# Seven products instead of eight in the mixers' second gates and in retention's output product

## The chip, the cores and the metric

The kernel runs on one core of one Trainium2 chip. The metric is the device time of one execution in microseconds (us). Of the kernel before there are three runs: 2315.1, 2315.0 and 2314.92 us, median 2315.0 us.

## The reference, cut to what matters

One decoder layer on 256 tokens of width 2048, in float32. Two half feed-forward blocks stand around a pair of token mixers that work side by side, and a gated embedding follows. The change touches the mixers only:

```python
rq, rk, rv, rg, aq, ak, av, gate_r, gate_a = jnp.split(h @ w_in[i], SPLIT_POINTS, axis=-1)
...
ro = head_group_norm(retention_chunkwise(rq, rk, rv), ret_gn_g[i]).astype(h.dtype)
ret_branch = (jax.nn.silu(rg) * ro) @ w_ret_out[i]
...
att_branch = sliding_window_attention_sinks(aq, ak, av, att_sinks[i]) @ w_att_out[i]

mixed = (jax.nn.sigmoid(gate_r) * ret_branch + jax.nn.sigmoid(gate_a) * att_branch) @ w_mix_out[i]
```

`gate_r`, `gate_a`, `w_ret_out` and `w_mix_out` are 2048 by 2048; `w_att_out` is 1024 by 2048, since attention has 16 heads of 64.

## The kernel before, in words

Every float32 product is made of three matmuls. A weight chunk of 128 x 1024 floats (512 KB) is loaded by the queue of SyncE (line 105), ACT rounds it to a high part (line 91), DVE subtracts to get the low part (line 92), and PE adds low x high, high x high and high x low into one PSUM bank (lines 291 to 293, in `Sum.add`). The activations are split into high and low parts in the same way. A chunk that covers 512 columns and two blocks of 128 rows of the weight ("a single") feeds two token halves, so it costs PE 2 x 2 x 3 = 12 matmuls of 128 x 512.

The feed-forward blocks already use a second form. `Seven` takes the two chunks of one pair of row blocks for two neighbouring column blocks, and treats tokens x rows times rows x columns as a product of 2 x 2 blocks, which is done with seven products in place of eight (a scheme of Strassen's kind). PE runs 7 x 3 = 21 matmuls where two singles take 24. For that DVE makes four sums of weight blocks (lines 163 to 166) and three and a half low parts of 1024 where two singles need two; ACT rounds three and a half times. The left side needs sums of the activations as well (`seven_forms`, lines 362 to 365, and a split). At the end of a column pair a fold of four additions (lines 373 to 376) joins the common products, and four more additions (line 794 in the feed-forward) join the plain ones. `block` runs such a column pair: a list of units, "P" for a pair of singles and "S" for a seven, with four PSUM banks for the plain sums and four for the common ones, eight in all, which is the whole PSUM.

All instructions are recorded in program order and each engine runs its own in that order. `plan` is the list of all weights in the order of use. `fill` runs ahead of PE: it loads and splits weights as long as less than `ahead` = 45 matmuls of work lie ready, fewer than 90 are loaded, and the count of buffers that the stage granted (`slots_for_weights`) is not used up. A single holds two of these buffers, a seven holds seven and needs eight while it is made. There are 46 in all, and the activations lie in the same pool. Smaller work (the heads of retention and attention, transposes) stands in the list `side`; one entry is run after each unit of weights (`run_side`).

In the mixers the order is: retention's values, queries and keys, retention's gate (tiles `rg`), attention's queries and keys (`aqk`, five groups of four chunks), attention's values (`av`), then the second gates (`gt`, eight blocks of 512 columns with eight singles each). While the `gt` blocks run, the side list takes the eight pairs of attention heads, each in four parts: scores `att1` (tiles `as`, DVE maxima), exponentials `att1b` on ACT, scaling `att1c` on DVE, transposes `att2` (tiles `at`), and the product with the values `att3` (tiles `ao`, then `attt`). ACT copies each gate out of PSUM (`sig`, line 1182). Then for each of four column blocks come retention's output product (`mr`, eight singles) and attention's (`ma`, four singles); DVE multiplies each by its gate (lines 1207, 1211), adds them (1212), and the sum is transposed into `mixt` (line 1198) for the last product (`mo`).

Of the kernel before, what the change touches and what calls it, by code (L numbers as in the profile page):

```python
# [15 lines left out]
P = 128  # L16
# [32 lines left out]
def layer(ctx: ExitStack, tc: tile.TileContext, io):  # L49
# [13 lines left out]
    def banks(name):  # L63
        return [bank(name + str(j)) for j in range(2)]
# [290 lines left out]
    def seven_forms(full, hi, lo):  # L355
# [10 lines left out]
        split(hi, lo, raw)  # L366
        return lambda e: [(hi[:, 2 * j + e, :], lo[:, 2 * j + e, :]) for j in range(4)]

    def seven_common(p1, p6, p7, q5):

        e, w = slot([P, 2, 512], F32, "eve"), slot([P, 2, 512], F32, "evw")
        act.copy(e[:, 0], p1)
        dve.tensor_tensor(w[:, 0], e[:, 0], p6, ALU.add)
# [315 lines left out]
    def gu_units(j):  # L689
        if j == 0:  # L690
            return [("P", p) for p in range(KD // 2)]
        order = "PPSSPSSP" if j % 2 == 0 else "PPSPSPSP"
        sevens = list(SEVEN[: order.count("S")])
        plain = [p for p in range(KD // 2) if p not in sevens]
        return [(kind, (sevens if kind == "S" else plain).pop(0)) for kind in order]

    def gu_keys(name, j):
        return lambda n, p: (name + "_gu", j, n, p)
# [198 lines left out]
    def plan_mixers():  # L897
        plan_tokens(("w_rv", 0), KD)
        for grp in range(8):
            plan_features([("w_in_f", grp)], KD)  # L900
        for blk in range(1, 4):
            plan_tokens(("w_rv", blk), KD)
        for grp in range(8, 16, 2):
            plan_tokens(("w_in_f2", grp), KD)
        for grp in range(16, 21):
            plan_features([("w_in_f", grp)], KD)
        plan_tokens(("w_av",), KD, nk=4)
        for grp in range(21, 37, 2):
            plan_tokens(("w_in_f2", grp), KD)
        for j in range(0, 8, 2):  # L910
            plan_tokens(("w_ret2", j), KD)
            plan_tokens(("w_att2", j), KD // 2)
        for blk in range(4):
            plan_tokens(("w_mix", blk), KD)

# [6 lines left out]
    def mixers(ht, norm, residual, keepers, away):  # L922
# [142 lines left out]
        for j in range(5):  # L1065
            ps = banks(f"aqk{j}")
            features_out([(("w_in_f", grp), ps)], KD, both_halves)
            grp += 1
            dst = akv[:, 0:2, :] if j == 4 else aq[j // 2][:, j % 2 * 2 : j % 2 * 2 + 2, :]
            rotate(ps, f"ra{j}", dst, cos_a, sin_a, SH_A)  # L1070
# [4 lines left out]
        assert not side or len(side) < 3  # L1075
        run_side(len(side))

        att_t = []

        def att1(m):  # L1080
            def f():
                c = m // 4
                q, k = aq[c][:, m % 4, :], akv[:, c, :]
                ps = banks(f"as{m}")
                for e in range(2):
                    r = slice(e * DH, (e + 1) * DH)
                    pe.matmul(ps[e][:, :P], q[r, :P], k[r, :P], start=True, stop=True)
                    pe.matmul(ps[e][:, P:384], q[r, P:], k[r, :], start=True, stop=True)
# [12 lines left out]
                es = small.tile([P, 2, 2], F32, tag="aes", name=f"aes{m}")  # L1101
                dve.tensor_tensor(es, skb, mx, ALU.subtract)
                keep["a", m] = s, nm, es
            return f

        def att1b(m):
            def f():
                s, nm, es = keep["a", m]
                act.activation(es, es, AF.Exp)
                sm = small.tile([P, 2, 2], F32, tag="asm", name=f"asm{m}")  # L1110
                for t in range(2):
                    for e in range(2):
                        x = s[:, e, :P] if t == 0 else s[:, e, P:]
                        act.activation(
                            x, x, AF.Exp, bias=nm[:, t, e : e + 1], accum_out=sm[:, t, e : e + 1]
                        )
                keep["b", m] = sm
            return f

        def att1c(m):  # L1120
            def f():
                (s, nm, es), sm = keep.pop(("a", m)), keep.pop(("b", m))
                dve.tensor_tensor(sm, sm, es, ALU.add)
                dve.reciprocal(sm, sm)
                for t in range(2):
                    for e in range(2):
                        x = s[:, e, :P] if t == 0 else s[:, e, P:]
                        dve.tensor_scalar(x, x, sm[:, t, e : e + 1], None, ALU.mult)
                keep["p", m] = s
            return f  # L1130
# [14 lines left out]
        def att3(m):  # L1145
# [16 lines left out]
                    dve.tensor_tensor(d[r, S:], ps[e][r, :S], d[r, :S], ALU.subtract)  # L1162
# [12 lines left out]
        sig = []  # L1175
        for j in range(8):
            ps = banks(f"gt{j}")
            paired_out(("w_in_f2", grp), KD, rhs, ps)
            grp += 2
# [3 lines left out]
        run_side(len(side))  # L1183

        mix_t = []
        y = {}
# [5 lines left out]
        def turned(v, kk):  # L1192
# [5 lines left out]
                    pe.transpose(ps[:, j, t * P : (t + 1) * P], v[:, t, (kk + j) * P : (kk + j + 1) * P], ident)  # L1198
            split(mt[:, :, :S], mt[:, :, S:], ps)

        for j in range(4):
            for v in (sig[j], sig[4 + j]):
                act.activation(v, v, AF.Sigmoid)
            pr = banks(f"mr{j}")
            paired_out(("w_ret2", 2 * j), KD, lambda k: of_pairs(ret_t, k), pr)
            for t in range(2):
                dve.tensor_tensor(sig[j][:, t], sig[j][:, t], pr[t], ALU.mult)
            pa = banks(f"ma{j}")
            paired_out(("w_att2", 2 * j), KD // 2, lambda k: of_pairs(att_t, k), pa)
            for t in range(2):  # L1210
                dve.tensor_tensor(sig[4 + j][:, t], sig[4 + j][:, t], pa[t], ALU.mult)
            dve.tensor_tensor(sig[j], sig[j], sig[4 + j], ALU.add)
            later(1, lambda v=sig[j]: turned(v, 0))
            later(2, lambda v=sig[j]: turned(v, 2))

        stats = small.tile([P, 2, 4, 6], F32, tag="stats", name="mixst", bufs=1)

# [232 lines left out]
```

## Time and profile before

| what | us |
|---|---|
| median of three runs | 2315.0 |
| the profiled execution | 2312.8 |
| its span, first to last instruction | 2311.0 |
| PE busy | 2279.6 |
| DVE busy | 1871.4 |
| ACT busy | 1162.9 |

The profiled execution is 2.2 us shorter than the median. Its span leaves out 1.8 us before the first and after the last instruction. Busy time of an engine is the time in which at least one of its instructions was running; PE's matmuls overlap, so a busy PE says that it never stood still, and not how many matmuls it could have done. The stages of the change lie between 1072.3 us (first `gt` matmul) and 1402.9 us (first `mo` matmul).

### The profile page before, as it was taken

What the parts mean: (1) busy time and instruction counts of PE and PEld (TensorE: products, weight loads), DVE (VectorE), ACT (ScalarE), POOL (GpSimd) and SP (SyncE); (2) the same over time, 40 slices, a digit from 0 to 9 for tenths busy, and PEclk for the clock granted to TensorE, in tenths of its full rate; (3) what the DMA queues carried; (4) which work ended last, traced back from release to release, by engine and by line L of the source; (5) the groups of instructions that cost most, each with busy time, mean ns of one, the idle gap of its engine ahead of it and who ended that gap; (6) DMA issues with size and microseconds to landing.
All of it is one profiled execution on the core that took longest, in us unless ns stands there. A gap on an engine that the chain in (4) does not pass through costs nothing.

```text
span 2311.0 us, 28634 instructions
## 1 busy us (share of the span) xinstructions
PE 2279.6 (99%) x10502; PEld 1887.7 (82%) x10502; DVE 1871.4 (81%) x2348; ACT 1162.9 (50%) x1404; POOL 97.0 (4%) x53
## 2 busy tenths in 40 slices
PE   9999999999999999999999999999999999999997
PEld 7788888888887888888778888888888888888876
DVE  7999999988988874677655555779999999889876
ACT  5555555565553342434554543355565555655432
POOL 0000000000000530133000000000000000000000
PEclk9999999999999999999999999999999999999999
DMA  9566666665587565546556667476666566565771
GB/s 316 164 218 191 194 208 194 197 218 182 201 287 263 176 225 160 170 150 198 159 158 183 184 207 260 161 249 207 192 191 212 182 204 217 172 219 193 289 255 55
DMA packets 193725, 465.70 MB, mean 202 GB/s; under 512 B 14768, under 2 KB 16048, under 8 KB 193584
## 3 DMA queue, kind: packets, MB, share of 16 engines
q1 hardware_dynamic: 191456, 460.91, 60.7%
q10 hardware_dynamic: 2128, 2.97, 0.4%
q8 instruction: 82, 1.34, 0.2%
q14 instruction: 59, 0.48, 0.1%
HBM read 455.43 MB, written 8.39 MB: 201 GB/s over the span
## 4 chain that ended last, share of the span: by engine, by line
PE 95%; DVE 3%; issue 1%; DMA 0%; ACT 0%; DVEq 0%; ACTq 0%
PE f2g L293 3%; PE f2g L291 3%; PE f2g L292 3%; PE f1g L291 3%; PE gt L291 3%; PE f1g L292 3%; PE f1g L293 3%; PE rqk L242 3%; PE gt L292 3%; PE gt L293 3%; PE f2u L291 2%; PE f2u L292 2%; PE f2u L293 2%; PE f1u L292 2%; PE f1u L291 2%; PE f1u L293 2%
## 5 line engine op out<-in xcount | busy, mean ns | idle before, releaser
L92 DVE TENSOR_TENSOR lf_gu<-rf_gu,hf_gu 128x1024 fp32r<-128x1024 f32 (+1 forms) x283 | 334.5, 1215 | 10.1 <-ACT hf_gu L91 9.7
L91 ACT CAST hf_gu<-rf_gu 128x1024 fp32r<-128x1024 f32 (+1 forms) x283 | 282.0, 1046 | 19.1 <-DMA rf_gu<-in_f_gu 18.8
L92 DVE TENSOR_TENSOR lw_in_f<-rw_in_f,hw_in_f 128x1024 fp32r<-128x1024 f32 x148 | 208.2, 1439 | 61.7 <-ACT hw_in_f L91 59.1
L92 DVE TENSOR_TENSOR lf_down<-rf_down,hf_down 128x1024 fp32r<-128x1024 f32 x152 | 180.9, 1221 | 28.2 <-ACT hf_down L91 23.2
L91 ACT CAST hf_down<-rf_down 128x1024 fp32r<-128x1024 f32 x152 | 155.5, 1051 | 77.7 <-DMA rf_down<-in_f_down 24.4
L91 ACT CAST huf_gu<-uf_gu 128x1024 fp32r<-128x1024 f32 x70 | 73.8, 1054 | 158.9 <-DVE uf_gu L164 153.2
L91 ACT CAST hw_in_f<-rw_in_f 128x1024 fp32r<-128x1024 f32 x148 | 145.8, 1051 | 0.2
L291 PE MATMUL f1g<-hf_gu,xt 128*128 128x512 f32 x247 | 97.3, 394 | 5.3 <-ACT hf_gu L91 5.3
L291 PE MATMUL gt<-hw_in_f,ht 128*128 128x512 f32 x256 | 102.5, 400 | 0.0
L292 PE MATMUL gt<-hw_in_f,ht 128*128 128x512 f32 x256 | 99.9, 390 | 0.0
L293 PE MATMUL gt<-lw_in_f,ht 128*128 128x512 f32 x256 | 99.9, 390 | 0.0
L292 PE MATMUL f1g<-hf_gu,xt 128*128 128x512 f32 x247 | 96.9, 392 | 0.0
L293 PE MATMUL f1g<-lf_gu,xt 128*128 128x512 f32 x247 | 96.8, 392 | 0.0
L291 PE MATMUL f2g<-hf_gu,ht 128*128 128x512 f32 x247 | 96.5, 391 | 0.0
L293 PE MATMUL f2g<-lf_gu,ht 128*128 128x512 f32 x247 | 96.2, 389 | 0.0
L292 PE MATMUL f2g<-hf_gu,ht 128*128 128x512 f32 x247 | 96.1, 389 | 0.0
L91 ACT CAST hvf_gu<-vf_gu 128x1024 fp32r<-128x1024 f32 x70 | 73.8, 1055 | 29.7 <-DVE vf_gu L166 29.7
L92 DVE TENSOR_TENSOR luf_gu<-uf_gu,huf_gu 128x1024 fp32r<-128x1024 f32 x70 | 85.3, 1219 | 0.0
L92 DVE TENSOR_TENSOR lvf_gu<-vf_gu,hvf_gu 128x1024 fp32r<-128x1024 f32 x70 | 85.3, 1218 | 0.0
L795 ACT ACTIVATE eve<-eve 128x1024 f32<-128x1024 f32 x20 | 21.2, 1062 | 127.0 <-DVE eve L794 127.0
L291 PE MATMUL f2u<-hf_gu,ht 128*128 128x512 f32 x212 | 83.5, 394 | 0.0
L291 PE MATMUL f1u<-hf_gu,xt 128*128 128x512 f32 x212 | 83.3, 393 | 0.0
(1053 smaller groups left out, 6275.1 us busy)
## 6 DMA issues: line engine op xcount, KB each, us to landing
rf_gu<-in_f_gu SPq DMA_DIRECT2D x351, 512.0 KB, 5.0
rf_down<-in_f_down SPq DMA_DIRECT2D x176, 512.0 KB, 4.5
rw_in_f<-in_w_in_f SPq DMA_DIRECT2D x148, 512.0 KB, 4.1
rw_rv<-in_w_rv SPq DMA_DIRECT2D x32, 512.0 KB, 4.4
rw_ret<-in_w_ret SPq DMA_DIRECT2D x32, 512.0 KB, 4.2
rw_mix<-in_w_mix SPq DMA_DIRECT2D x32, 512.0 KB, 4.5
rw_pg<-in_w_pg SPq DMA_DIRECT2D x32, 512.0 KB, 4.8
rw_att<-in_w_att SPq DMA_DIRECT2D x16, 512.0 KB, 4.1
```

Source lines behind the costliest of these rows:

```text
L91: act.copy(dst_hi, src)
L92: (lo_engine or dve).tensor_tensor(dst_lo, src, dst_hi, ALU.subtract)
L242: pe.matmul(ps[f], hi[:, kk, f * P : (f + 1) * P], rhs(k), start=k == 0, stop=k == n_k - 1,)
L291: pe.matmul(o, al, bh, start=first, stop=False)
L292: pe.matmul(o, ah, bh, start=False, stop=False)
L293: pe.matmul(o, ah, bl, start=False, stop=self.left == 0)
L795: act.activation(g, g, AF.Silu)
```

## The change

Of the second gates the first four blocks stay as they are. The last four become two column pairs (`ga0`, `ga1`) run by `block`, each with four pairs of singles and four sevens in the order P P S S P S S P. Retention's output product becomes two column pairs (`mr0`, `mr1`) with six pairs of singles and two sevens each, in the order P P P S P S P P. So twelve pairs of singles turn into twelve sevens. The sums of the activations that the sevens need are made once for each group of four row blocks: two groups of the layer's input during the third and fourth gate block, one group of retention's result after the second `ma` block (`forms_of`, which first adds high and low parts back together in `whole`).

The order of the work changes too. Attention's values and keys are computed before its queries. The eight head pairs of attention are spread over 40 units (the last two query groups and the four plain gate blocks) where they had 57 before, and each pair has four units between its scores and its transposes where it had five. All four blocks of attention's output product now run ahead of retention's. The buffers granted to the weights are 18 in the plain gates, 22 in the gate pairs and 20 in the output products; before, 14 were granted from the queries and keys on up to the last product.

```diff
+    def whole(parts, name):
+        full = slot([P, 4, S], F32, name)
+        n = 4 // len(parts)
+        for j, v in enumerate(parts):
+            dve.tensor_tensor(full[:, n * j : n * j + n], v[:, :, :S], v[:, :, S:], ALU.add)
+        return full
+
+    def forms_of(parts, name):
+        hi, lo = (slot([P, 8, P], F32R, name + w) for w in "hl")
+        return seven_forms(whole(parts, name + "w"), hi, lo)
...
+    GATE_UNITS = units_of("PPSSPSSP", (0, 1, 2, 3))
+    RET_UNITS = units_of("PPPSPSPP", (0, 1))
+    gate_keys = lambda b: lambda n, p: ("w_in_f2", 29 + 4 * b + 2 * n, p)
+    ret_keys = lambda b: lambda n, p: ("w_ret2", 4 * b + 2 * n, p)
...
-        for m in range(8):
-            side.append(att1(m))
-            side.append(att1b(m))
-            side.append(att3(m - 1) if m else idle)
-            side.append(att1c(m))
-            side.append(idle)
-            side.append(att2(m))
-            side.append(idle)
-        side.append(att3(7))
+        begin = [0, 5, 10, 15, 20, 24, 28, 32, 38, 39]
+        at = [[] for _ in range(40)]
+        for m in range(8):
+            for j, part in ((0, att1), (1, att1b), (2, att1c), (4, att2)):
+                at[begin[m] + j].append(part(m))
+            at[begin[m + 2]].append(att3(m))
+        side.extend((lambda jobs=jobs: [f() for f in jobs]) for jobs in at)
...
-        for j in range(8):
+        slots_for_weights(18)
+        for j in range(4):
+            def before(c, j=j):
+                if c == 0 and j >= 2:
+                    g = j - 2
+                    made[g] = forms_of([ht[:, 4 * g : 4 * g + 4, :]], f"gaf{g}")
             ps = banks(f"gt{j}")
-            paired_out(("w_in_f2", grp), KD, rhs, ps)
+            paired_out(("w_in_f2", 21 + 2 * j), KD, rhs, ps, before)
...
+        def mixer_block(name, units, keys, lhs):
+            ps = [banks(name + w) for w in "ab"]
+            got = []
+            block(name, units, keys, lhs, forms, block_sums(ps, units, KD), lambda *a: got.extend(seven_common(*a)))
+            for n in range(2):
+                for t in range(2):
+                    dve.tensor_tensor(got[n][:, t], got[n][:, t], ps[t][n], ALU.add)
+            return got
+
+        slots_for_weights(22)
+        for b in range(2):
+            sig += mixer_block(f"ga{b}", GATE_UNITS, gate_keys(b), rhs)
...
+        slots_for_weights(20)
         for j in range(4):
-            for v in (sig[j], sig[4 + j]):
-                act.activation(v, v, AF.Sigmoid)
-            pr = banks(f"mr{j}")
-            paired_out(("w_ret2", 2 * j), KD, lambda k: of_pairs(ret_t, k), pr)
-            for t in range(2):
-                dve.tensor_tensor(sig[j][:, t], sig[j][:, t], pr[t], ALU.mult)
+            v = sig[4 + j]
+            act.activation(v, v, AF.Sigmoid)
             pa = banks(f"ma{j}")
             paired_out(("w_att2", 2 * j), KD // 2, lambda k: of_pairs(att_t, k), pa)
...
+            if j == 1:
+                made[0] = forms_of(ret_t[:2], "mrf")
+        for b in range(2):
+            for v in sig[2 * b : 2 * b + 2]:
+                act.activation(v, v, AF.Sigmoid)
+            pr = mixer_block(f"mr{b}", RET_UNITS, ret_keys(b), lambda k: of_pairs(ret_t, k))
+            for n in range(2):
+                j = 2 * b + n
+                dve.tensor_tensor(sig[j], sig[j], pr[n], ALU.mult)
+                dve.tensor_tensor(sig[j], sig[j], sig[4 + j], ALU.add)
+            side.append(idle)
+            side.extend(lambda v=v, kk=kk: turned(v, kk) for v in sig[2 * b : 2 * b + 2] for kk in (0, 2))
```

More of the change, by code (lines that the diff above doesn't have):

```diff
@@ L367, in seven_forms, with units_of, block_sums @@
         return lambda e: [(hi[:, 2 * j + e, :], lo[:, 2 * j + e, :]) for j in range(4)]
+    def whole(parts, name):
[7 more added lines that the diff above has]
+        return seven_forms(whole(parts, name + "w"), hi, lo)
+    def units_of(order, sevens):
+        sevens = list(sevens)
+        plain = [p for p in range(KD // 2) if p not in sevens]
+        return [(kind, (sevens if kind == "S" else plain).pop(0)) for kind in order]
+    def block_sums(ps, units, n_k):
+        s = sum(kind == "S" for kind, p in units)
+        return [[Sum(ps[t][n], n_k - (2 * s if t and n else s)) for n in range(2)] for t in range(2)]
     def seven_common(p1, p6, p7, q5):
@@ L692, in gu_units @@
         order = "PPSSPSSP" if j % 2 == 0 else "PPSPSPSP"
-        sevens = list(SEVEN[: order.count("S")])
-        plain = [p for p in range(KD // 2) if p not in sevens]
-        return [(kind, (sevens if kind == "S" else plain).pop(0)) for kind in order]
+        return units_of(order, SEVEN[: order.count("S")])
     def gu_keys(name, j):
@@ L904, in plan_mixers @@
             plan_tokens(("w_in_f2", grp), KD)
-        for grp in range(16, 21):
+        plan_tokens(("w_av",), KD, nk=4)
+        for grp in (20, 16, 17, 18, 19):
             plan_features([("w_in_f", grp)], KD)
-        plan_tokens(("w_av",), KD, nk=4)
-        for grp in range(21, 37, 2):
+        for grp in range(21, 29, 2):
             plan_tokens(("w_in_f2", grp), KD)
+        for b in range(2):
+            block_units(GATE_UNITS, gate_keys(b))
         for j in range(0, 8, 2):
-            plan_tokens(("w_ret2", j), KD)
             plan_tokens(("w_att2", j), KD // 2)
+        for b in range(2):
+            block_units(RET_UNITS, ret_keys(b))
         for blk in range(4):
@@ L1064, in mixers @@
         akv = slot([P, 4, S], F32, "akv")
[L1065 to L1070, printed above, removed]
         ps = banks("av")
@@ L1074, in mixers, with attention_features @@
             dve.tensor_copy(akv[:, 2 + t, :], ps[t][:, :S])
-        assert not side or len(side) < 3
-        run_side(len(side))
+        def attention_features(grp):
+            j = grp - 16
+            ps = banks(f"aqk{j}")
+            features_out([(("w_in_f", grp), ps)], KD, both_halves)
+            dst = akv[:, 0:2, :] if j == 4 else aq[j // 2][:, j % 2 * 2 : j % 2 * 2 + 2, :]
+            rotate(ps, f"ra{j}", dst, cos_a, sin_a, SH_A)
+        for grp in (20, 16, 17):
+            attention_features(grp)
+        assert not side
         att_t = []
@@ L1163, in att3 @@
             return f
+        begin = [0, 5, 10, 15, 20, 24, 28, 32, 38, 39]
+        at = [[] for _ in range(40)]
         for m in range(8):
-            side.append(att1(m))
-            side.append(att1b(m))
-            side.append(att3(m - 1) if m else idle)
-            side.append(att1c(m))
-            side.append(idle)
-            side.append(att2(m))
-            side.append(idle)
-        side.append(att3(7))
-        sig = []
-        for j in range(8):
+            for j, part in ((0, att1), (1, att1b), (2, att1c), (4, att2)):
+                at[begin[m] + j].append(part(m))
+            at[begin[m + 2]].append(att3(m))
+        side.extend((lambda jobs=jobs: [f() for f in jobs]) for jobs in at)
+        for grp in (18, 19):
+            attention_features(grp)
+        made = {}
+        forms = lambda p: made[p // 2](p % 2)
+        slots_for_weights(18)
+        sig = []
+        for j in range(4):
[3 more added lines that the diff above has]
+                    made[g] = forms_of([ht[:, 4 * g : 4 * g + 4, :]], f"gaf{g}")
             ps = banks(f"gt{j}")
-            paired_out(("w_in_f2", grp), KD, rhs, ps)
-            grp += 2
+            paired_out(("w_in_f2", 21 + 2 * j), KD, rhs, ps, before)
             sig.append(slot([P, 2, 512], F32, f"sig{j}"))
@@ L1182, in mixers @@
                 act.copy(sig[-1][:, t], ps[t])
-        run_side(len(side))
+        assert not side
+        def mixer_block(name, units, keys, lhs):
[7 more added lines that the diff above has]
+        slots_for_weights(22)
+        for b in range(2):
+            sig += mixer_block(f"ga{b}", GATE_UNITS, gate_keys(b), rhs)
         mix_t = []
@@ L1210, in mixers @@
             for t in range(2):
[L1211 to L1214, printed above, removed]
+                dve.tensor_tensor(v[:, t], v[:, t], pa[t], ALU.mult)
+            if j == 1:
+                made[0] = forms_of(ret_t[:2], "mrf")
+        for b in range(2):
+            for v in sig[2 * b : 2 * b + 2]:
[7 more added lines that the diff above has]
+            side.extend(lambda v=v, kk=kk: turned(v, kk) for v in sig[2 * b : 2 * b + 2] for kk in (0, 2))
         stats = small.tile([P, 2, 4, 6], F32, tag="stats", name="mixst", bufs=1)
```

## The prediction

> **What bounds the kernel now.** I read the page first, then busy time by stage, then PE's waits, then the timeline around the change. Engines, and the chain that ended last:
>
> ```profile
> PE 2279.6 (99%) x10502; PEld 1887.7 (82%) x10502; DVE 1871.4 (81%) x2348; ACT 1162.9 (50%) x1404; POOL 97.0 (4%) x53
> ...
> PE 95%; DVE 3%; issue 1%; DMA 0%; ACT 0%; DVEq 0%; ACTq 0%
> ```
>
> The set end is a PE that hardly ever stands still. By stage (columns: stretch, its length, busy us of PE, PE's weight load, DVE, ACT, POOL; clock; DMA share; GB/s) the first two rows are the eight gate blocks, the third the output products, the fourth a stretch of the second feed-forward, which is made of sevens already:
>
> ```profile
> 1072.30:1171.00 98.70, 98.70 (x478) 77.73 (x477) 57.19 (x99) 48.05 (x97) 0.00 (x0) 1.00 0.55 169
> 1171.00:1269.50 98.50, 98.50 (x471) 78.40 (x470) 54.54 (x86) 48.05 (x85) 0.00 (x0) 1.00 0.57 173
> 1269.50:1402.90 133.40, 133.40 (x601) 110.46 (x600) 73.28 (x72) 61.41 (x66) 0.00 (x0) 1.00 0.65 202
> 1600.00:1700.00 100.00, 100.00 (x451) 83.02 (x450) 95.14 (x111) 57.73 (x67) 0.00 (x0) 1.00 0.64 204
> ```
>
> In the stage of the change PE has no gap at all in 330.6 us, at full granted clock; DVE works 185.0 us of them, ACT 157.5. So a matmul taken out there comes off the end, as long as the extra DVE work stays under PE. The last row shows that a stage of sevens can keep PE full with DVE at 95%. PE's waits (us in total, times, longest) name for the sevens of the whole kernel only these:
>
> ```profile
> PE f12s L291 <- ACT f1a L745: 1.0, 1, 1.0
> PE f11s L293 <- DVE luf_gu L92: 0.7, 1, 0.7
> ...
> PE f11s L293 <- DVE lvf_gu L92: 0.2, 1, 0.2
> ```
>
> **What a matmul is worth.** A matmul's recorded duration is 0.39 us, but they overlap; its price is the distance of starts:
>
> ```profile
> 1254.74 0.39 PE L292 MATMUL gt<-hw_in_f,ht 128*128 128x512 f32 x1
> ...
> 1269.25 0.39 PE L293 MATMUL gt<-lw_in_f,ht 128*128 128x512 f32 x1
> ```
>
> Between these starts lie 64 matmuls of the same kind with nothing in between: 14.51 / 64 = 0.2267 us each. A seven takes 21 where two singles take 24. Twelve sevens (4 + 4 + 2 + 2) take away 36 matmuls: 36 x 0.2267 = 8.16 us. PE's other instructions (attention, transposes) stay the same in number, 10122 against 10086 rows in all. That is the whole gain, and its upper bound.
>
> **What DVE and ACT get.** DVE in the second feed-forward, running without a break (start, us, line, operation, tiles, shapes, count):
>
> ```profile
> 1606.14 0.68 DVE L163 TENSOR_TENSOR uf_gu<-rf_gu,rf_gu 128x512 f32<-128x512 f32 x1
> ...
> 1612.81 0.69 DVE L163 TENSOR_TENSOR uf_gu<-rf_gu,rf_gu 128x512 f32<-128x512 f32 x1
> ...
> 1619.54 4.63 DVE L92 TENSOR_TENSOR lf_gu<-rf_gu,hf_gu 128x1024 fp32r<-128x1024 f32 x4
> 1624.08 0.68 DVE L373 TENSOR_TENSOR evw<-eve,f22s 128x512 f32<-128x512 f32 x1
> ...
> 1626.80 2.35 DVE L92 TENSOR_TENSOR lf_gu<-rf_gu,hf_gu 128x1024 fp32r<-128x1024 f32 x2
> 1629.07 1.28 DVE L794 TENSOR_TENSOR eve<-eve,f2g 128x512 f32<-128x512 f32 x2
> ...
> 1631.65 1.23 DVE L796 TENSOR_TENSOR evw<-eve,evw 128x1024 f32<-128x1024 f32 x1
> ```
>
> One seven costs DVE 6.67 us (first to second row) and 6.73 (to the third), say 6.70; a single's low part (1624.08 - 1619.54) / 4 = 1.135; a fold 1626.80 - 1624.08 = 2.72; the four last additions 1631.65 - 1629.07 = 2.58 at most. Over the stage DVE gets 12 x (6.70 - 2 x 1.135) = 53.2 for the sevens, 4 x (2.72 + 2.58) = 21.2 for folds and additions, and three times the left-hand sums. Those are in the trace too:
>
> ```profile
> 1528.75 0.42 DVE L362 TENSOR_TENSOR sums<-keep 128x256 f32<-128x256 f32 x1
> ...
> 1529.88 0.42 DVE L365 TENSOR_TENSOR sums<-keep,sums 128x256 f32<-128x256 f32 x1
> ```
>
> 1.55 us, and one addition of 1024 before and one low part behind, 2 x 1.14: 3.8 us each, 11.5 in all. Sum +86 us: about 271 of 322 us. It fits on the average. ACT gets 12 x 1.6 us of casts and loses gate copies: some 178 us of 322. Both extras are hidden under PE, worth nothing at the end while they are early enough. Where that is tight:
>
> The two gate pairs. PE needs 2 x (4 x 24 + 4 x 21) = 360 matmuls, 81.6 us. In the recorded order of the changed kernel DVE cannot start the first seven before the last attention copies, which wait for the last `ao` matmul just before the first pair; that takes about 1.6 us: the matmul's 0.39, then one ACT copy and two of DVE:
>
> ```profile
> L1162 DVE TENSOR_TENSOR attt<-ao,attt 64x256 fp32r<-64x256 f32 x16 | 6.8, 422 | 2.3 <-ACT attt L1161 1.7
> ...
> L1161 ACT CAST attt<-ao 64x256 fp32r<-64x256 f32 x16 | 5.9, 367 | 8.4 <-PE ao L1155 8.1
> ```
> From there it must have made eight sevens, ten singles, one fold and one set of additions when PE comes to the low part of the last seven's second half, 323 matmuls on, at 73.2 us: 1.6 + 53.6 + 11.4 + 2.72 + 2.58 = 71.9. There is 1.3 us to spare in 73. I take no stall from this, but it is the thinnest cover in the change. Behind the pairs attention's output product is all singles, 1.135 us of DVE per 12 x 0.2267 = 2.72 us of PE, so that a lag is made good there; retention's pairs have only two sevens each.
>
> Loads. The number of bytes and of DMA issues (885 rows on SP in both) does not change. In the pairs, followed along DVE's account above, a raw chunk can be issued at the least 43 matmuls, 9.7 us, before DVE wants it (the last seven). From issue to landing:
>
> ```profile
> DMA to landing us min/median/max: 3.6/4.9/7.5
> ```
>
> (the feed-forward's chunks, 1600 to 1700 us). Hidden.
>
> Attention's side work, closer together. Before, the scaled scores are ready well ahead of the transposes that read them:
>
> ```profile
> 1128.90 1.01 DVE L1128 TENSOR_SCALAR asc<-asc,asm 128x128 f32<-128x128 f32 x4
> ...
> 1133.62 0.82 PE L1138 MATMUL at<-ident,asc 128*128 128x128 f32 x6
> ```
>
> 1133.62 - 1129.91 = 3.7 us. Transposes now stand one unit (2.72 us) nearer to the scores, but the scaling too is recorded one unit earlier, so that the margin should stay near 3.7; if DVE, being busier, does not follow, it is 1.0. The left-hand sums fall on the starts of the third and fourth gate block, where head pairs 5 and 7 begin. I cost this at nothing, with the bound 2 x (3.8 - 1.0) = 5.6 us.
>
> Handing over PSUM banks, and transposing the mixed result. After each `mr` pair the first transposes wait for the last additions, one product and one sum: 0.4 + 0.69 + 2 x 1.23 = 3.5 us (durations of the same shapes above), and two units, 24 x 0.2267 = 5.4 us, stand between. Hidden; if not, two times at most 2 us. Moving `ma` ahead of `mr` costs nothing: attention's results are done before the gate pairs, retention's long before.
>
> I set 0.1 us of stall for each pair, from the waits above (1.9 us for the twenty seven-made column pairs of gates and ups in both feed-forwards): 0.4 us. Sum: -8.16 + 0.4 = -7.8 us. The profiled execution has 2312.8 us (span 2311.0 and 1.8 around it) and would have 2305.0; the median of the runs lies 2.2 us higher, and so the prediction is 2315.0 - 7.8 = 2307.2 us. About 0.2%, 4.6 us, is what a measurement can tell from no change.
>
> **The rivals.** First, DVE becomes the bound in the gate pairs. The overlap of DVE's operations, which gave 6.70 us, may not hold there. With the mean durations of single instructions:
>
> ```profile
> L92 DVE TENSOR_TENSOR lf_gu<-rf_gu,hf_gu 128x1024 fp32r<-128x1024 f32 x30 | 35.7, 1220 | 0.3 <-ACT hf_gu L91 0.3
> ...
> L165 DVE TENSOR_TENSOR vf_gu<-rf_gu,uf_gu 128x512 f32<-128x512 f32 x9 | 6.2, 692 | 0.8 <-DVE uf_gu L164 0.5
> ```
>
> a seven is 3 x 1.22 + 5 x 0.69 = 7.11, and the account above 1.6 + 56.9 + 12.2 + 2.76 + 2.76 = 76.2 against 73.2: a stall of 3.0 us, 2310.2. For it: DVE was idle for 4.9 of 100 us even in the feed-forward stretch, and such holes in front of folds find only 1.3 us of cover here. Against: the timeline shows no hole inside a run of sevens. The Trainium skill (VectorE: DVE Perf Modes, "The DRAIN you can't avoid") says that the next operation does not start until the pipe of the one before has emptied; by that rule the account goes by full durations and this rival is the forecast. The trace does not agree where no operand is handed on: 4 low parts of 1.22 us take 4.63 us, not 4.88.
>
> Second, the denser attention stalls PE at the transposes of pairs 5 and 7, by 5.6 us: 2312.8. Against: the scaling is moved along with them.
>
> Third, slower: buffers. In the second gate pair the weights of all four sevens are recorded only when PE reaches them, since 22 buffers are used up; before, the lead was mostly 42 matmuls or more and never under 28. If a seven's splits had to wait for buffers that PE has just let go, each would cost PE up to DVE's 6.70 us: 4 x 6.70 = 26.8, or 2315.0 - 7.8 + 26.8 = 2334.0. It decides from 2.0 us for each seven on (7.8 / 4). Against: the waits in the recorded order go to buffers that are older, released 38 to 59 matmuls (8.6 to 13.4 us) ahead of use, which is more than one seven's chain. For: two sevens stand next to each other, and 38 matmuls cover one seven (6.70) and not two.
>
> **How the numbers follow.** Forecast, no stall above 1.5 us: 0.62. DVE bound in the pairs: 0.20, between 2308.7 and 2312, so 0.12 faster and 0.08 same. Attention or bank waits: 0.07, of which 0.02 faster and 0.05 same. Buffers: 0.11, slower. So faster 0.62 + 0.12 + 0.02 = 0.76, same 0.13, slower 0.11. The range starts at 2306.0 (8.16 us and 0.8 of spread between executions and fewer changes between side work and gates) and ends at 2313.0, above the first two rivals; it leaves out the third and a little below.
>
> **What the profile after would show.** Right: PE's matmul count lower by 36, no new wait of `ga` or `mr` on DVE above 1 us, the stretch from the first gate matmul to the first `mo` matmul (attention's last two query groups aside) shorter by 8 us, DVE at 97% or more in the gate pairs. Wrong by DVE: waits of `ga..s` banks on `luw_in_f` or `lvw_in_f`, in the last seven of each pair first. Wrong by attention: waits of `at` on `asc`. Wrong by buffers: the same waits on weights, but with DVE idle in front of them for PE or for the queue of SP.

## The result, and the profile after

The changed kernel takes 2305.48 us (median of five runs, 2303.17 to 2305.83), the kernel before 2315.0 us beside it (five runs). The ratio is 0.9959, with a 95% interval of 0.9944 to 0.9973: faster by 0.41%. The forecast was 2307.2 us with a range of 2306.0 to 2313.0. The direction and the mechanism were right, the gain was 9.5 us and not 7.8, and the time lies 0.5 us below the range. A second measurement, among the experiments, gave 2304.05 us and a ratio of 0.9953 (0.9941 to 0.9966), a gain of 11.1 us over the 2315.11 beside it. The profiled execution took 2305.66 us, 0.2 us above the median; that of before was 2.2 us below its own, so the two profiles must be compared by stage and not by their spans.

The page of the changed kernel, engines and the chain that ended last:

```profile
PE 2271.7 (99%) x10466; PEld 1882.5 (82%) x10466; DVE 1945.0 (84%) x2467; ACT 1184.4 (51%) x1427; POOL 96.0 (4%) x53
...
PE 95%; DVE 3%; DMA 1%; issue 0%; ACT 0%; SPq 0%; ACTq 0%; DVEq 0%
```

PE has 36 rows fewer (10466 against 10502), DVE is busy 73.6 us longer, ACT 21.5, and PE still sets the end. The stages of the changed kernel (stretch, its length, busy us of PE, weight load, DVE, ACT, POOL; clock; DMA share; GB/s): the four plain gate blocks, the first and second gate pair, attention's output product, and retention's pairs:

```profile
1077.60:1182.50 104.90, 104.90 (x531) 82.35 (x529) 77.72 (x147) 59.51 (x124) 6.46 (x3) 1.00 0.48 147
1182.50:1223.30 40.80, 40.80 (x185) 33.49 (x185) 39.07 (x47) 25.95 (x31) 0.00 (x0) 1.00 0.65 207
1223.30:1264.90 41.60, 41.60 (x185) 34.47 (x184) 41.05 (x50) 26.78 (x29) 0.00 (x0) 1.00 0.66 219
1264.90:1308.70 43.80, 43.80 (x195) 36.26 (x194) 28.90 (x34) 21.89 (x24) 0.00 (x0) 1.00 0.64 201
1308.70:1395.00 86.30, 86.30 (x390) 71.42 (x389) 71.56 (x80) 41.23 (x46) 0.00 (x0) 1.00 0.65 219
```

PE has no gap in any of them, at full granted clock. DVE works 96% of the first gate pair and 99% of the second. PE's waits (us in total, times, longest) name no tile of the gates, of attention or of the output products; among the longest, and those of the feed-forward's sevens, are:

```profile
PE lnps L509 <- DVE f1y L502: 5.3, 3, 4.8
...
PE f12s L291 <- ACT f1a L766: 1.0, 1, 1.0
...
PE f11s L293 <- DVE luf_gu L92: 0.4, 1, 0.4
```

The first line was 3.5 us in all and 2.8 at the longest in the profile of before. It belongs to the norm behind the first feed-forward, which the change does not touch; the last of the experiments is about it.

How near DVE came to PE in the second gate pair is in the timeline. Its last low part of the last seven, and PE's first use of it (start, us):

```profile
1253.84 1.22 DVE L92 TENSOR_TENSOR lvw_in_f<-vw_in_f,hvw_in_f 128x1024 fp32r<-128x1024 f32 x1
```

```profile
1256.81 0.39 PE L293 MATMUL ga1s<-lvw_in_f,gaf1h 128*128 128x512 f32 x1
```

It ends at 1255.06, 1.75 us ahead. The prediction had 1.3.

**Where the time went.** Since PE never waits in the stage, the distance from the start of each matmul to that of the next, added up by tile, divides its length without remainder. The stretch runs from the first matmul of attention's queries, keys or values to the first `mo` matmul. The middle column is the first experiment: the order of the changed kernel (and its buffer counts) with no seven in it.

| us, start to start | before | new order, no sevens | after |
|---|---|---|---|
| second gates (`gt`, `ga`) | 179.21 | 176.62 | 171.16 |
| retention's output (`mr`) | 87.81 | 87.56 | 84.84 |
| attention's output (`ma`) | 43.52 | 43.52 | 43.52 |
| `aqk` and `av` | 68.11 | 68.60 | 68.60 |
| transposes `at` | 4.58 | 5.27 | 5.38 |
| transposes `mxt` | 2.13 | 1.42 | 1.42 |
| other heads' work | 17.44 | 17.44 | 17.44 |
| **the stretch** | **402.79** | **400.42** | **392.35** |
| last product, `mo` | 87.78 | 88.75 | 88.75 |

From the third column to the second it is the sevens: 8.07 us. From the second to the first it is the order: 2.37 us, of which the last product gives back 0.97, because eight transposes of the mixed result now stand behind the first `mo` matmuls. 8.07 + 2.37 - 0.97 = 9.47 us, against 9.52 between the medians here and 11.1 in the second measurement. The sum is a reading of three profiles; the medians are too coarse to bear out its tenths.

### The profile page after: what moved, and what is told of

It reads as the page before. It is cut to its first block, busy times and chain, and to the rows that moved or that the text cites. A ratio compares the mean times of both kernels' runs of the same rounds, so it can differ in the third digit from the quotient of the medians.

```text
span 2303.6 us, 28759 instructions
## 1 busy us (share of the span) xinstructions
PE 2271.7 (99%) x10466; PEld 1882.5 (82%) x10466; DVE 1945.0 (84%) x2467; ACT 1184.4 (51%) x1427; POOL 96.0 (4%) x53
## 4 chain that ended last, share of the span: by engine, by line
PE 95%; DVE 3%; DMA 1%; issue 0%; ACT 0%; SPq 0%; ACTq 0%; DVEq 0%
PE f2g L293 3%; PE f2g L291 3%; PE f2g L292 3%; PE f1g L291 3%; PE f1g L292 3%; PE f1g L293 3%; PE rqk L242 3%; PE f2u L292 2%; PE f2u L291 2%; PE f2u L293 2%; PE f1u L291 2%; PE f1u L293 2%; PE f1u L292 2%; PE aqk L242 2%; PE f2d L291 2%; PE f1d L291 2%
## 5 line engine op out<-in xcount | busy, mean ns | idle before, releaser
L92 DVE TENSOR_TENSOR lw_in_f<-rw_in_f,hw_in_f 128x1024 fp32r<-128x1024 f32 x140 | 195.6, 1427 | 29.3 <-ACT hw_in_f L91 27.1
L91 ACT CAST hw_in_f<-rw_in_f 128x1024 fp32r<-128x1024 f32 x140 | 138.9, 1051 | 2.3 <-DMA rw_in_f<-in_w_in_f 2.0
L291 PE MATMUL f2u<-hf_gu,ht 128*128 128x512 f32 x212 | 83.5, 394 | 0.0
L291 PE MATMUL f1u<-hf_gu,xt 128*128 128x512 f32 x212 | 83.3, 393 | 0.0
L292 PE MATMUL f2u<-hf_gu,ht 128*128 128x512 f32 x212 | 82.5, 389 | 0.0
L293 PE MATMUL f2u<-lf_gu,ht 128*128 128x512 f32 x212 | 82.5, 389 | 0.0
L292 PE MATMUL f1u<-hf_gu,xt 128*128 128x512 f32 x212 | 82.5, 389 | 0.0
```

The costliest lines, as they stand in the source:

```text
L91: act.copy(dst_hi, src)
L92: (lo_engine or dve).tensor_tensor(dst_lo, src, dst_hi, ALU.subtract)
L291: pe.matmul(o, al, bh, start=first, stop=False)
L292: pe.matmul(o, ah, bh, start=False, stop=False)
L293: pe.matmul(o, ah, bl, start=False, stop=self.left == 0)
```

## The experiments

All twelve compute the whole layer. Two of them do some work twice, and nothing is left out of any. Times beside each other come from the same chip: the kernel before had a median of 2314.2 us for the first four (21 runs), 2314.66 for the next four (21) and 2315.11 for the last four (15). "The stretch" is that of the table.

Theory A says that the sevens are worth their 36 matmuls and the rest comes from how often side work (heads of 128-wide matmuls) breaks PE's run of 512-wide ones. In theory B the places of the side work do not matter.

### The order alone

Every "S" is a "P" again, in the gates and in retention's output, in the order of the changed kernel; without sevens no forms and folds are made.

```diff
-    GATE_UNITS = units_of("PPSSPSSP", (0, 1, 2, 3))
-    RET_UNITS = units_of("PPPSPSPP", (0, 1))
+    GATE_UNITS = units_of("PPPPPPPP", ())
+    RET_UNITS = units_of("PPPPPPPP", ())
```

> The changed kernel with every seven turned back into singles: same order of work, same list of side work, same column pairs. Stage = from the first matmul of attention's queries, keys or values to the first mo matmul; 402.8 us before, 392.4 us after. Theory A (each break of a run of 512-wide matmuls by side work costs PE about 0.21 us, and the new list has 15 breaks where the old had 24; eight transposes of mixt also move behind the first mo matmul): the stage is about 2.2 us shorter than before, some 400.5 us, and 8.2 us longer than after. Theory B (the order is worth nothing on PE and the sevens gave all of it): the stage is as before, 402.8 less 0.7 for the moved transposes, and a seven is worth more than 0.68 us.

Measured: 2313.06 us (ten runs), ratio 0.9995 (0.9985 to 1.0004), the stretch 400.42 us. By time alone the order can't be told from no change; by the stretch it is 2.37 us shorter, where the trace repeats to some hundredths (the stage before it, from the first matmul of retention's gate on, takes 101.94 to 101.97 us in all these kernels). The sevens are worth 400.42 - 392.35 = 8.07 us, for 36 matmuls of 0.2267 (8.16).

### Retention's sevens taken back alone

```diff
-    RET_UNITS = units_of("PPPSPSPP", (0, 1))
+    RET_UNITS = units_of("PPPPPPPP", ())
```

> The changed kernel with retention's output product in singles; the gates keep eight sevens. By 0.2267 us for each of 12 matmuls the stage is 2.7 us longer than after, 395.1 us (theory A). By theory B, where twelve sevens carry the whole 10.4 us less 0.7, four of them carry 3.2: 395.6 us.

Measured: 2306.22 us, ratio 0.9963 (0.995 to 0.9976), the stretch 395.11. That is 2.76 above 392.35, for 12 matmuls (2.72). So each seven gave about what its three matmuls are worth, in the gates (8.07 - 2.76 = 5.31 for 24, worked out 5.44) and in retention's output alike, and nothing was paid in stalls.

### The side work apart, and joined in the kernel before

In the changed kernel, the attention part `att3` is moved off the unit on which scores of another pair stand:

```diff
-            at[begin[m + 2]].append(att3(m))
+            at[begin[m + 2] + (2 if m < 6 else 0)].append(att3(m))
```

> The changed kernel with the attention product of six head pairs run two units after the scores of a later pair and not together with them: six breaks more in PE's run. Theory A: the stage is 6 x 0.21 = 1.3 us longer than after, 393.7 us. Theory B: 392.4 us, unchanged.

Measured: 2305.86 us, ratio 0.9964 (0.995 to 0.9978), the stretch 393.34, 0.99 longer. The run of `gt` matmuls is broken 18 times instead of 12. In the kernel before, the reverse:

```diff
-            side.append(att3(m - 1) if m else idle)
+            side.append(idle)
             side.append(att1c(m))
             side.append(idle)
-            side.append(att2(m))
+            side.append(both(att3(m - 1), att2(m)) if m else att2(m))
```

> The kernel before, no sevens and the old order, with the attention product of seven head pairs run together with the transposes of the next pair: seven breaks fewer. Theory A: the stage is 7 x 0.21 = 1.5 us shorter than before, 401.3 us. Theory B: 402.8 us.

Measured: 2312.76 us, ratio 0.9995 (0.9986 to 1.0004), the stretch 401.67, 1.12 shorter, with 18 breaks in `gt` instead of 25. So six breaks more cost 0.99 us and seven fewer gain 1.12: 0.16 us each, in both directions and in two kernels, less than the 0.21 that theory A had used but not nothing as in B. The trace of before shows where the cost lies, here at one break:

```profile
1133.38 0.39 PE L293 MATMUL gt<-lw_in_f,ht 128*128 128x512 f32 x1
1133.62 0.82 PE L1138 MATMUL at<-ident,asc 128*128 128x128 f32 x6
1134.19 0.48 PE L291 MATMUL gt<-hw_in_f,ht 128*128 128x512 f32 x1
1134.50 0.40 PE L292 MATMUL gt<-hw_in_f,ht 128*128 128x512 f32 x1
1134.74 0.40 PE L293 MATMUL gt<-lw_in_f,ht 128*128 128x512 f32 x1
```

From the first matmul behind the transposes to the next it is 0.31 us, then 0.24; about a dozen matmuls on, the distances are 0.2267 again. Why the first ones are longer is not shown. In the table the gates lose 25 - 13 = 12 breaks and 2.59 us, of which the transposes `at` give 0.69 back: 1.90 us, or 0.16 for each of the twelve. The rest of the order's effect (`aqk` and `av` 0.49 longer, `mr` 0.26 shorter) no experiment takes apart.

### Buffers

The gate pairs get 18 buffers in place of 22, which makes the lead of the weights shorter. This asks for the third rival.

```diff
-        slots_for_weights(22)
+        slots_for_weights(18)
```

> The changed kernel with 18 buffers for the weights in the gate pairs and not 22, less work ahead and no more work. The last wait goes 38 matmuls (8.6 us) ahead of use with 22; four buffers are two singles, 24 matmuls, so that some 14 matmuls or 3.2 us stay for a seven's 6.7 us on DVE. The theory of the third rival: 3 us or more for each of several sevens, stage 400 to 420 us. The other: recorded leads say little, since the buffers that are reused are old ones; stage within 2 us of 392.4.

Measured: 2304.86 us, ratio 0.9957 (0.9942 to 0.9973), the stretch 394.12, 1.77 longer. PE's waits in the pairs are small:

```profile
PE ga1s L293 <- DVE luw_in_f L92: 0.8, 1, 0.8
PE ga1s L293 <- DVE lvw_in_f L92: 0.2, 1, 0.2
```

Even with four buffers fewer the price is 1.8 us in the stretch, too little for the medians to show, and not the 26.8 of the rival: the waits for buffers are met early enough. The granted clock stays at 1.00 behind these two waits.

### How thin DVE's cover is

A low part of the sevens in the gate pairs is computed a second time into the same place, once in every second seven (four in all), and in a second kernel in all eight. Each copy costs DVE one subtraction of 128 x 1024.

```diff
             a.make()
+            if nm.startswith("w_in_f2") and self.key[2] % 2:
+                dve.tensor_tensor(a.lo, a.raw, a.hi, ALU.subtract)
```

> The changed kernel with one low part of 1024 computed a second time in four of the eight sevens of the gate pairs: 4 x 1.135 = 4.5 us more of DVE, nothing else. In the profile after, the low part of the last seven's second half ends 1.75 us before PE takes it (predicted: 1.3). If this is the whole cover, the two pairs get 4.5 - 1.75 = 2.8 us longer, with PE waiting on low parts of the last sevens; stage 395.2 us against 392.4. If DVE has more room than the account says (buffers or loads hold it back in places where it could run ahead), the stage stays under 393.4.

> The same in all eight sevens: 9.1 us more of DVE. DVE's account: 9.1 - 1.75 = 7.3 us longer, stage 399.7 us, nearly all of what the sevens gave. With more room than the account: less than 397.

Measured: four copies 2309.11 us, ratio 0.9973 (0.9963 to 0.9984), the stretch 396.92, 4.57 us longer; eight copies 2313.94 us, ratio 0.9996 (0.9985 to 1.0006), the stretch 401.43, 9.08 longer. The stretches expected were shorter (395.2 and 399.7). The waits are where the prediction's first rival put them, in the last seven of each pair first; with four copies:

```profile
PE ga1s L295 <- DVE lw_in_f L175: 1.0, 1, 1.0
...
PE ga1s L295 <- DVE luw_in_f L92: 0.8, 1, 0.8
...
PE ga0s L295 <- DVE lvw_in_f L92: 0.2, 1, 0.2
```

They sum to 2.0 us as idle time; by the distances of starts PE lost 2.7. Four copies of 1.135 us are 4.54, and less the 1.75 of spare 2.79: so far the account holds. What was not expected stands behind the two waits, in PE's timeline and in the windows of the same kernel:

```profile
1257.34 0.50 PE L295 MATMUL ga1s<-lw_in_f,ht 128*128 128x512 f32 x1 [1.03 <-DVE lw_in_f L175]
...
1259.08 0.73 PE L295 MATMUL ga1s<-luw_in_f,gaf1h 128*128 128x512 f32 x1 [0.77 <-DVE luw_in_f L92]
1259.60 0.63 PE L293 MATMUL ga1s<-hvw_in_f,gaf1l 128*128 128x512 f32 x1
1260.03 0.63 PE L294 MATMUL ga1s<-hvw_in_f,gaf1h 128*128 128x512 f32 x1
```

```profile
1255.00:1259.00 4.00, 2.28 (x9) 1.24 (x7) 3.96 (x5) 4.00 (x5) 0.00 (x0) 1.00 1.02 382
1259.00:1262.60 3.60, 3.52 (x9) 2.69 (x10) 3.60 (x5) 3.50 (x5) 0.00 (x0) 0.53 0.56 175
1262.60:1270.00 7.40, 7.40 (x34) 6.11 (x33) 7.26 (x9) 6.87 (x7) 0.00 (x0) 1.00 0.85 295
```

After 1.0 and 0.8 us of idling the granted clock is 0.53 over 3.6 us, that is, half for 3.4 us of them, and the starts stand 0.43 us apart instead of 0.2267: from 1259.08, eight distances take 3.51 us instead of 1.81. 2.7 + 1.7 = 4.4 of the 4.57. With eight copies it is 6.2 us by distances and 2.8 at the low clock, 9.0 of 9.08. So the cover of DVE is as thin as the prediction said, and a lag can cost PE clearly more than its own length. That 4.54 us more of DVE's time cost 4.57 in the stretch is chance: 2.7 of it are the lag and 1.7 the clock. The Trainium skill (TensorE: Matmul & The Clock Gate, Part 1) has the clock at half after at least one idle window of about 3.4 us; here 1.8 us of idling in two pieces was enough, and the time at the low clock, 3.4 us, is as long as such a window.

### More sevens in retention's output

Three instead of two per pair, with forms for a second group of rows:

```diff
-    RET_UNITS = units_of("PPPSPSPP", (0, 1))
+    RET_UNITS = units_of("PPPSPSSP", (0, 1, 2))
...
-            if j == 1:
-                made[0] = forms_of(ret_t[:2], "mrf")
+            if j in (1, 2):
+                made[j - 1] = forms_of(ret_t[2 * j - 2 : 2 * j], f"mrf{j}")
```

> The changed kernel with three sevens and not two in each of retention's output pairs, order PPPSPSSP. DVE has room there: 6 matmuls fewer, 6 x 0.2267 = 1.4 us, stage 391.0 us. If the sums of the second group of retention's result or the transposes of the mixed result come in the way, the stage is 392.4 or longer, with PE waiting on mr sums or low parts.

Measured: 2302.66 us (2300.27 to 2303.88), ratio 0.9946 (0.9929 to 0.9963), the stretch 391.04, 1.31 shorter for six matmuls (1.36). No new wait. With four per pair, `units_of("PPPSSPSS", (0, 1, 2, 3))`:

> Four sevens in each of retention's pairs, two of them last in each, in the order P P P S S P S S; the norm as in the changed kernel. Theory A (a matmul is worth 0.2267 us while DVE keeps up): 12 matmuls less than the changed kernel, 2.72 us, the stretch takes 389.6 us and the time is 2302.5 us. Rival one in this place (DVE bounds where sevens follow one another, and the fold, the additions and the mixed sum queue behind the last two): waits of the second pair's banks on the low parts of the output weights above 1 us, and a stretch of 391 us or more, not better than with three.

Measured: 2310.7 us (11 runs), ratio 0.9983 (0.9974 to 0.9992), the stretch 398.29, where A had 389.6. So the twelve matmuls less are lost again and 6 us more. The rival was right in naming DVE and the mixed sum, and wrong in naming the output weights' low parts. PE's two long waits are for the mixed sum, and for a PSUM bank of the second pair that DVE's reading of the transposes (`mixt`) has to free:

```profile
PE mxt L1253 <- DVE sig L1273: 2.6, 1, 2.6
...
PE mr1s L291 <- DVE mixt L92: 2.3, 1, 2.3
```

DVE's timeline of this kernel shows the making of both:

```profile
1343.17 4.62 DVE L92 TENSOR_TENSOR lw_ret<-rw_ret,hw_ret 128x1024 fp32r<-128x1024 f32 x4
1347.71 0.68 DVE L396 TENSOR_TENSOR evw<-eve,mr0s 128x512 f32<-128x512 f32 x1
...
1354.06 1.23 DVE L1273 TENSOR_TENSOR sig<-sig,eve 128x1024 f32<-128x1024 f32 x1
...
1373.85 1.22 DVE L92 TENSOR_TENSOR lvw_ret<-vw_ret,hvw_ret 128x1024 fp32r<-128x1024 f32 x1
1374.98 0.68 DVE L92 TENSOR_TENSOR mixt<-mxt,mixt 128x512 fp32r<-128x512 f32 x1
```

With the sevens at the end of the pair, the fold of the pair is taken up at 1347.71, after PE has ended it (the second pair's first matmul starts at 1347.14), and the first mixed sum, the tenth operation from there, is done at 1355.3, when PE has used up its two units and waits. In the changed kernel the fold is done before the pair's end (1339.67 starts its last addition, and the pair's last matmul starts at 1350.65), so that none of it is left to do there. DVE does not catch up, and reads the last transposes at 1374.98, behind the parts of the next seven; until then their bank is taken. After both waits the clock falls; over the 4 us behind the first it is 0.60, half for 3.2 of them:

```profile
1356.00:1360.00 4.00, 4.00 (x12) 3.16 (x12) 3.97 (x5) 2.05 (x3) 0.00 (x0) 0.60 0.03 9
```

2.6 + 2.3 us of waits and two times eight matmuls at nearly double distance (16 x 0.2 = 3.2 us) are 8.1 of the 8.7 us that are missing. Four sevens with a "P" last, as in the gates' order, were not tried; that the loss comes from their place at the end and not from their number is read from the timeline.

### The norm between the executions

Executions of one kernel differ by up to 5.8 us (2311.7 to 2317.5 in 15 runs of the kernel before), which is more than half of the gain. In the traces one stage differs most: from the last matmul of the first feed-forward's down product to the first of retention's values. It takes 12.4 to 12.7 us in six profiles (before among them) and 14.2 to 15.5 us in six others (after among them), whatever the edit was. In the timeline of before, DVE goes through the last low parts of the value weights, made ahead, and then the norm's additions (ACT's row is the rounding of the last chunk but one):

```profile
699.03 1.05 ACT L91 CAST hw_rv<-rw_rv 128x1024 fp32r<-128x1024 f32 x1 [1.11 <-DMA rw_rv<-in_w_rv]
...
702.27 1.23 DVE L92 TENSOR_TENSOR lw_rv<-rw_rv,hw_rv 128x1024 fp32r<-128x1024 f32 x1 [0.94 <-PE f1e L292]
703.42 0.68 DVE L870 TENSOR_TENSOR f1y<-f1y,f1e 128x512 f32<-128x512 f32 x1
```

and after:

```profile
701.76 1.05 ACT L91 CAST hw_rv<-rw_rv 128x1024 fp32r<-128x1024 f32 x1 [2.98 <-DMA rw_rv<-in_w_rv]
...
702.85 2.53 DVE L92 TENSOR_TENSOR lw_rv<-rw_rv,hw_rv 128x1024 fp32r<-128x1024 f32 x2 [2.73 <-ACT hw_rv L91]
705.30 0.68 DVE L891 TENSOR_TENSOR f1y<-f1y,f1e 128x512 f32<-128x512 f32 x1
```

ACT, waiting for the load, rounded this chunk 2.7 us later, and the norm, queued on DVE behind the low parts, began 1.9 us later; PE then waited 4.8 us and not 2.8 for its transposes, and the clock was at half for 6.8 us from 709.5 on and not for 3.4 from 709.7 on. Theory C says that this landing is the spread between executions, theory D that it is not. The test makes two of these low parts later than the norm:

```diff
-        last_ahead = 136
+        last_ahead = 112 if i == 0 else 136
...
-        slots_for_weights(27, last_ahead, last_ahead + 24)
+        slots_for_weights(27, last_ahead, 160)
```

> The changed kernel once more, beside the next one on the same chip. Both theories: 2303.2 to 2305.8 us, median near 2305.3. From the last matmul of the first feed-forward's down product to the first one of retention's values it takes about 15.0 us when the weight DMA of the last chunk made ahead lands late, about 12.5 when it lands early.

> The changed kernel, but two chunks of retention's value weights fewer are rounded and split ahead of the norm behind the first feed-forward, so that DVE's queue in front of the norm holds no subtraction that waits for the last of the loads. Theory C (the 2 to 3 us between executions, and 2.2 of the distance between the profiled execution and the median before, come from a DMA landing that DVE's subtraction waits for, with the norm queued behind it): the stretch from the last down matmul to the first matmul of the values takes at most 12.7 us, and the median is about 2303 us, 2 to 2.5 below the changed kernel's. Theory D (the landing is not it, PE's clock or something else is): the stretch is 12.5 or 15 us as before and the median stays at 2305.3. A mishap for both: the two subtractions, now behind the norm's first half, come late for the values, and the stretch grows to 17 us or more (two of 1.22 us each).

Measured on one chip: the changed kernel 2304.05 us (2302.91 to 2306.56), the other 2304.39 us (2303.28 to 2304.64), ratio 0.9953 each. The stage up to the first value matmul took 14.43 us in the one and 8.96 in the other, and PE's wait for the norm is gone:

```profile
PE rv L291 <- ACT hw_rv L91: 1.4, 1, 1.4
...
PE lnps L509 <- DVE f1y L502: 1.1, 3, 0.4
...
PE rv L293 <- DVE lw_rv L92: 0.6, 1, 0.6
```

But the values then take 3.9 us more (183.54 against 179.65 us up to retention's gate): the two chunks that were put behind the norm are late there, in their high part (the first of these lines) and their low part (the last), and behind these waits the clock is at half for 3.4 us. The gain was given back at another place. Theory C is borne out as far as the stage goes, and the spread of five runs fell from 3.65 to 1.36 us, which is few runs; its 2 us of gain are not. The landing is not the whole of the spread either: in the fourteen profiles the second feed-forward, which no edit touches, takes 700.9 to 702.1 us from its first matmul to its last, and the last product (`pg`) 95.4 to 96.6.

The last kernel has three sevens in retention's pairs and this edit:

> Three sevens instead of two in each of retention's pairs, and the two chunks fewer ahead of the norm. Theory A (36 matmuls were worth 8.07 us, so 6 more less are worth 1.36 us): the stretch from attention to the last product takes 391.0 us, and with theory C the time is 2303.0 - 1.4 = 2301.6 us; with theory D it is 2302.7 as without the second edit.

Measured: 2303.07 us (2301.95 to 2303.55), ratio 0.9947 (0.9935 to 0.996), the stretch 390.98. The stretch agrees with A; of C's gain from the norm there is none, as in the kernel before it. The one with three sevens and the norm as it was has the lowest median, 2302.66 us, but with ratios of 0.9946 and 0.9947 the two can't be told apart. Their intervals overlap that of the changed kernel too, and only the stretch tells them from it.

## Why the prediction was right in kind and too high

- **A matmul is worth 0.2267 us, twelve sevens 8.16.** Right: 8.07, and 2.76 of them for retention's 12 (2.72 worked out).
- **"That is the whole gain, and its upper bound."** This is the step that failed. The prediction counted PE's instructions, found their number unchanged outside the sevens, and had no term for their order. The new order was worth 1.40 us: 2.37 in the stretch, less 0.97 in the last product. The trace of before showed it: 768 `gt` matmuls took 179.21 us start to start, where 768 x 0.2267 is 174.11, and the 5.10 between them stand at 25 breaks by side work, at the matmul before each and the dozen behind it. It was named for the range's low end only, together with the spread, at 0.8 us for both.
- **0.4 us of stall for the four pairs.** None came. With these three terms the time is 2315.0 - 8.07 - 1.40 = 2305.53; measured 2305.48. That it agrees so closely is partly luck, since medians of the kernel before on different chips lay between 2314.2 and 2315.1, and the changed kernel's second measurement gained 11.1 us.
- **The range.** Its low end stood at the full gain of the matmuls and 0.8 us. Order and spread were each larger than that, so that a forecast which was right in its main term still missed.
- **DVE's account of the gate pairs,** 71.9 of 73.2 us, was right, with 1.75 us of spare against 1.3, and the kernels with doubled subtractions show that it was thin: of 4.54 us more of DVE's time, 2.7 came out as waits of PE. The first rival did not come: one seven takes DVE from 1184.80 to 1191.48 in the changed kernel, 6.68 us, against 6.70 in the account and 7.11 in the rival, so operations that hand nothing on overlap here too, where the Trainium skill's rule (VectorE: DVE Perf Modes, "The DRAIN you can't avoid") lets each wait for the one before; the section adds that a next operation that is not held starts earlier, which fits this trace:

```profile
1184.80 0.69 DVE L163 TENSOR_TENSOR uw_in_f<-rw_in_f,rw_in_f 128x512 f32<-128x512 f32 x1
...
1191.48 0.68 DVE L163 TENSOR_TENSOR uw_in_f<-rw_in_f,rw_in_f 128x512 f32<-128x512 f32 x1
```

- **Attention closer together, the second rival,** costs nothing: no wait of `at` on `asc`. The prediction looked there for a loss, and it was the place of the gain, since scores and outputs of two head pairs now share a break.
- **Buffers, the third rival:** no wait, and 1.8 us when four buffers are taken away.
- **Handing over the mixed sum,** 3.5 us within 5.4: hidden, as said. With sevens put last in the pair it is not, and the kernel with four loses by it.
- **Two small figures** change nothing: the pages count 10502 and 10466 matmuls where the prediction has 10122 and 10086 rows, 36 apart either way, and ACT's terms, 157.5 + 12 x 1.6, give 176.7 us at most and not 178.

## What to carry to other kernels

Where one engine is full, price its instructions by the distance of starts, and do so for the whole stage: what the sum of the plain instructions leaves over belongs to the breaks between kinds, and an order that has fewer of them is a gain of its own. Spend the other engine's spare time up to the last microsecond only where it can catch up before the next fold, and keep the costly operations away from the end of a block, where their results are wanted at once. Ask of the range what a bare rearrangement and the spread between executions could add, each as its own term.

## What the runs showed of the hardware

- The granted clock falls to about half after short waits too. 1.0 and 0.8 us of idling within 2.8 us, and a wait of 2.6 us, were each followed by 3.4 us at half clock, with the matmuls 0.43 us apart instead of 0.2267. In the kernel with four copies 2.7 us of waits cost 4.4. In all fourteen profiles, every fall of the clock between the first 12 us and the last matmul had at least 1.78 us of idling in the 3.4 us before it; idling of up to 1.04 us within 3.4 us, such as the 0.8 and 0.2 us of the kernel with 18 buffers, had none. What lies between was not seen.
- A break of a run of 128 x 512 matmuls by the attention heads' smaller ones costs about 0.16 us beside that work's own time (0.99 us for six more, 1.12 for seven fewer).
- A chunk of weights that ACT could round only 2.7 us later in one execution than in another held up, through a subtraction that waits for it, work behind it in DVE's queue that does not need it (the norm, by 1.9 us).
